# The input's additions in the down products: one pause more before and after each, and a buffer taken per block

## The chip, the cores and the metric

The kernel runs on one core of a Trainium2 chip. The metric is the device time of one execution, in microseconds. Five engines work side by side, each through its own queue in order: TensorE (PE) multiplies, VectorE (DVE), ScalarE (ACT) and GpSimd (POOL) work on elements, and SyncE (SP) starts the transfers. They wait for one another only through semaphores.

## The reference, cut to what matters

One layer of an encoder for 1104 tokens (64 of one request, 16 learned ones and 1024 of another) of width 1024. It begins and ends with half a feed-forward block, added to its own input:

```python
def half_ffn(x, g, wg, wu, wd):
    h = rmsnorm(x, g)
    return x + 0.5 * ((jax.nn.silu(h @ wg) * (h @ wu)) @ wd)

# in the layer, D_MODEL = 1024, D_FF = 2816
xp = half_ffn(xp, ffn1_norm[l], ffn1_wg[l], ffn1_wu[l], ffn1_wd[l])
...                      # DeltaNet heads and latent attention, each added to xp
xp = half_ffn(xp, ffn2_norm[l], ffn2_wg[l], ffn2_wu[l], ffn2_wd[l])
```

The change touches only how `x +` is done, in both blocks. "Down products" are those with `wd`, 2816 to 1024.

## The kernel before, in words

Activations lie transposed: 128 features on the partitions, 1104 tokens along the free dimension, cut for the products into pieces of 336, 384 and 384 (`CH`). A float32 factor is split into a high and a low part, and each product is three passes (high·high, high·low, low·high).

**The down products** (`down`, L968) take the 2816 inner features as 22 slices of 128, two at a time: ten groups of two in the main loop, the last two in another. Within a group the loop runs over the 8 blocks of 128 output features (`m`). A block is 2 slices x 3 passes x 3 pieces = 18 matmuls into three PSUM banks of the eight there are. When it is done, `evac` (L972) adds half of each bank to the result `R` in SBUF: for the first group ACT writes `R`, for all later ones DVE does three additions (`SCALAR_TENSOR_TENSOR R<-bk,R`). A bank is free for a new block when its addition is done.

Beside that run `down_loads` (rows of `wd` into `raw`, split by ACT and DVE into `wh`/`wl` or into two tiles both called `wx`) and `inner_loads` (two slices of inner activations from DRAM, split into pairs that the trace calls `st`, `XH`/`XL` or `ih`/`il`). Both fall at the start of a group: four casts on ACT, four subtractions on DVE.

**The input** `x` lies in DRAM as 8 blocks of 128x1104 (`x0`). `input_rows` (L1120) is a task of its own: for each `m` it loads the block into the tile `xa` and has DVE add it to `R`. There is one `xa`, so a load can start only when the addition before has read it.

**What sets the order.** The program is written by coroutines (`Tasks`, L430). Each `yield` gives the earliest modelled time of the next step (a number, counted from now) and what it needs: flags and free buffers. `step` picks the ready task of lowest rank, and the instructions go into each engine's queue in that order, for good. Times come from a small model (`Clock`), whose clock is TensorE's. `note` (L361) computes when an instruction would begin: from when its inputs are made, and, for a tile newly taken from a pool, from when the tile that had its place was last used. A tile that is merely written again has no such term. `nc.lag(xa)` is the modelled time until the load has landed. What the engines do at run time is set by the queues and by semaphores, which order load and addition on `xa` in either version.

`input_rows` waits for the flags `("R", m)` (`evac` of the first group has written block m) and `("R", m, 1)` (a later group has). It has rank 9, behind the products' helpers. All instructions are recorded under L424, the line of the helper that issues them, so tiles tell them apart.

Of the kernel before, what the change touches and what calls it, by code (L numbers as in the profile page):

```python
# [8 lines left out]
F32 = mybir.dt.float32  # L9
# [8 lines left out]
P = 128  # L18
# [6 lines left out]
T_ = NS + NM + NPR  # L25
# [784 lines left out]
def plain_steps(s, js, W, x, ready, tmp, hd, done):  # L810

    nc, T = s.nc, s.tasks
    V, A = nc.vector, nc.scalar
    hbs = []

    def gated(e, c, bs):
        yield 0, "sg"
        T.take("sg")
        t = tmp.tile([P, s.tw], F32, tag="sg", name="sg", bufs=CAPS["sg"])[:, :F]
        A.activation(t, bs[0][:, :F], AF.Silu)  # L820
        T.free("b")
        yield nc.lag(t), lambda: nc.complete(bs[1]) if len(bs) > 1 else None
        if not c:
            T.take("hb")
            hbs.append(tmp.tile([P, 2 * F], F32, tag="hb", name="hb", bufs=CAPS["hb"]))
        V.tensor_tensor(hbs[e][:, F * c:F * c + F], bs[1][:, :F], t, ALU.mult)
        T.free("b", "sg")
        if c:
            yield nc.lag(hbs[e])
            nc.sync.dma_start(hd[js[e]][:, :2 * F], hbs[e])  # L830
            T.free("hb", of=hbs[e])
            done.add((js[e], 0), nc.complete(hbs[e]) + 3.0)
    for c, e in [(0, 0), (0, 1), (1, 0), (1, 1)] + [(c, e) for e in js[2:] for c in (0, 1)]:
        bs = []
        for n in "AB":
            yield 0, "b", nc.when(W, (e, n))
            b = grab(s)
            for k in range(8):
                op = (0, 1, 7, 2)[2 * c + k // 4]
                if k % 4 == 0:  # L840
                    yield 0, ready.wait((0, op))
                mm3(nc, b[:, :F], [w[:, k * P:k * P + P] for w in W[e, n]], (x.h[op][:, k % 4, :], x.l[op][:, k % 4, :]), k == 0, k == 7)
            bs.append(b)
            if n == "A":
                T.add(gated(e, c, bs), -1)
        if c:
            T.free("A", "TS"[e % 2])
# [120 lines left out]
def down(s, R, fl, W, hs, free, last_group, after, chunks):  # L968

    nc, T = s.nc, s.tasks  # L970

    def evac(g, m, bs):  # L972
        for c, (o, w) in enumerate(CH):
            if g:
                nc.vector.scalar_tensor_tensor(R[:, m, o:o + w], bs[c][:, :w], 0.5, R[:, m, o:o + w], ALU.mult, ALU.add)
            else:
                nc.scalar.activation(R[:, m, o:o + w], bs[c][:, :w], AF.Copy, scale=0.5)
            T.free("b")
            yield 0
        fl.add(("R", m) + (1,) * (g > 0))  # L980

    def ready(j):
        return nc.when(W, j), nc.when(hs, j)
    for g in range(0, NF - 2, 2):
        for m in range(8):
            yield (0, "b", "b", "b", *ready(g), *ready(g + 1))
            bs = [grab(s) for c in range(3)]
            for i in (0, 1):
                for n, (x, y) in enumerate(PASSES):
                    for c, (o, w) in enumerate(CH):  # L990
                        nc.tensor.matmul(bs[c][:, :w], W[g + i][x][:, m, :], hs[g + i][y][:, o:o + w], start=(i + n == 0), stop=(i == 1 and n == 2))
                if not i:
                    yield 0
            T.add(evac(g, m, bs), -1)
        T.free(*free(g))
    last_group()
    g = NF - 2
    for c in chunks:
        o, w = CH[c]
        for m in range(8):  # L1000
            yield (0, "b", *ready(g), *ready(g + 1))
            b = grab(s)
            for i in (0, 1):
                mm3(nc, b[:, :w], [t[:, m, :] for t in W[g + i]], [t[:, o:o + w] for t in hs[g + i]], i == 0, i == 1)
            T.add(after(c, m, b), -1)


class Seven:
# [108 lines left out]
    def freed(self, g):  # L1117
        return ["d" + self.KINDS[j] for j in (g, g + 1)] + ["ix" if g // 2 % 2 else "is"]

    def input_rows(self, xa):  # L1120

        nc, T = self.s.nc, self.s.tasks
        for m in range(8):
            nc.sync.dma_start(xa, self.o.x0[m])
            yield nc.lag(xa), self.flags.wait(("R", m))
            nc.vector.tensor_tensor(self.R[:, m, :], self.R[:, m, :], xa, ALU.add)
            yield 0, self.flags.wait(("R", m, 1))
        self.flags.add("x0")

    def flow(self):  # L1130
        s, o, E = self.s, self.o, self.E
        nc, T = s.nc, s.tasks
        yield from plain_steps(s, range(o.plain), self.W1, o.x[0], o.ready, o.wk, self.hd, self.done)
        self.flags.add("plain")
        yield from half_steps(s, self.seq, self.W1, o.x, o.ready, o.wk, self.hd, self.done, {E - o.plain - 1: self.first_pair_done, E - 2: lambda: self.flags.add("last step", nc.at["tensor"])}, o.plain)
        yield 0, lambda: 0.0 if 1 in self.Wd else None
        o.second.close(1)
        o.first.close(1)
        pr = o.second("R")
        self.R = pr.tile([P, 8, T_], F32, name="R")  # L1140
        T.add(self.input_rows(pr.tile([P, T_], F32, name="xa")), 9)
        o.rest()

        def before_last():
            assert "x0" in self.flags
            T.free("w", "w", "w")
            o.before_last()
        yield from down(s, self.R, self.flags, self.Wd, self.hs, self.freed, before_last, o.after, o.chunks)
# [1105 lines left out]
def layer_kernel(tc, cst, x_prompt, x_sample, cache_mla_ckv, cache_mla_krope, state_gdn, state_conv, meta,  # L2254
# [21 lines left out]
    with ExitStack() as ctx:  # L2276
# [164 lines left out]
        def latents():  # L2441
# [24 lines left out]
            state.add("keys")  # L2466
        T.add(mix(), -2)
        T.add(flow(), 100)
        T.add(latents(), 99)
        for h in range(H):  # L2470
# [241 lines left out]
```

## Time and profile before

| | |
|---|---|
| three runs | 2384.83, 2392.31, 2393.76 us; median 2392.31 |
| the profiled execution | 2391.09 us, its span 2389.3 us |
| mean granted TensorE clock | 0.981 |
| first block's down products, main loop | from 515.5 us, 24.2 us a group when nothing waits |
| second block's down products | second group from 2113.49 us, third from 2137.69 us |


The profiled execution spends 1.8 us outside its span. A busy share says little here: PE is busy nearly everywhere, so what counts is where it stands still and where its clock is lower. The granted clock has two levels, 1.2 GHz (0.5) and 2.4 GHz (1.0); a stretch's figure is the mean over it.

### The profile page before, as it was taken

The page shows a single profiled execution, that of the slowest core. Times are in us where ns is not written, and L with a number is a line of the kernel's source. Part 1 is how long each engine was busy: PE and PEld are TensorE (multiplying, and loading weights), DVE is VectorE, ACT ScalarE, POOL GpSimd, SP SyncE. Part 2 cuts the span into 40 slices and gives each one's busy share as a digit, 9 for nine tenths or more (in the row PEclk, how much of TensorE's full clock was granted, in tenths as well). Part 3 has the DMA queues.
Part 4 walks back from the last instruction along what each step waited for, and adds up shares of the span by engine and source line. Part 5 has one row for each costly group of instructions (what it writes and reads, how often), then busy time and mean ns, then how long its engine had stood idle before and what let it go on. Part 6 is the DMA issues. An engine that isn't in the chain of part 4 may idle for free.

```text
span 2389.3 us, 41529 instructions
## 1 busy us (share of the span) xinstructions
PE 2306.6 (97%) x16356; PEld 2279.0 (95%) x16356; DVE 1511.5 (63%) x3499; ACT 925.2 (39%) x2038; POOL 203.7 (9%) x488
## 2 busy tenths in 40 slices
PE   9999999998999999899998999899999999989998
PEld 8999999998999899899998998899999999989998
DVE  7754455566666757878877566567554445747676
ACT  5333333351211445545633555334333333531123
POOL 0000000000000403322345000000000000000002
PEclk9999999998999999999998999999999999999999
DMA  6322222353230331112122103633222222453212
GB/s 197 117 75 78 82 82 71 100 200 122 79 114 28 115 88 49 54 36 64 37 69 66 48 17 95 194 106 99 82 65 72 82 83 84 139 182 103 81 55 76
DMA packets 231044, 214.30 MB, mean 90 GB/s; under 512 B 18372, under 2 KB 202864, under 8 KB 230848
## 3 DMA queue, kind: packets, MB, share of 16 engines
q1 hardware_dynamic: 230832, 211.64, 28.5%
q8 instruction: 128, 2.10, 0.4%
q14 instruction: 68, 0.56, 0.1%
q10 hardware_dynamic: 16, 0.00, 0.0%
HBM read 159.05 MB, written 52.55 MB: 89 GB/s over the span
## 4 chain that ended last, share of the span: by engine, by line
PE 82%; DVE 9%; DMA 3%; ACT 2%; issue 2%; POOL 1%; SPq 0%; DVEq 0%; POOLq 0%; ACTq 0%
PE bk L424 82%; DMA xa<-x 2%; DVE s L424 1%; DVE cv L424 1%; DVE R L424 1%; DVE wl L424 1%; DVE rs_q L424 1%; POOL rs_q L424 0%; DVE rs_r L424 0%; DMA X<-in_w_out_dram 0%; ACT s L424 0%; DMA s<-in_w_out_dram 0%; SPq L424 0%; POOL cql L424 0%; ACT wh L424 0%
## 5 line engine op out<-in xcount | busy, mean ns | idle before, releaser
L424 PE MATMUL bk<-s,wh 128*128 128x276 f32 x3136 | 601.1, 290 | 5.1 <-ACT sn L424 2.4
L424 PEld LDWEIGHTS bk<-s,wh 128*128 128x128 f32 x3136 | 493.2, 188 | 6.5 <-ACT sn L424 2.6
L424 PE MATMUL bk<-s,wl 128*128 128x276 f32 x1568 | 449.3, 290 | 1.6 <-DVE wl L424 1.6
L424 PE MATMUL bk<-s,wx 128*128 128x276 f32 x2964 | 394.0, 290 | 1.7 <-DVE s L424 1.7
L424 PEld LDWEIGHTS bk<-s,wx 128*128 128x128 f32 x2964 | 383.5, 188 | 1.9 <-DVE s L424 1.9
L424 DVE SCALAR_TENSOR_TENSOR R<-bk,R 128x384 f32<-128x384 f32 (+1 forms) x480 | 230.7, 533 | 131.7 <-PE bk L424 130.6
L424 PEld LDWEIGHTS bk<-s,wl 128*128 128x128 f32 x1568 | 293.5, 188 | 2.1 <-DVE wl L424 2.1
L424 DVE TENSOR_TENSOR sn<-bk,sn 128x276 f32<-128x276 f32 x237 | 105.0, 444 | 205.6 <-PE bk L424 201.7
L424 ACT COPY sn<-bk 128x276 f32<-128x276 f32 x237 | 91.9, 389 | 243.7 <-PE bk L424 240.7
L424 PE MATMUL bk<-XH,wh 128*128 128x384 f32 (+1 forms) x576 | 166.5, 343 | 0.0
L424 PE MATMUL bk<-XL,wh 128*128 128x384 f32 (+1 forms) x576 | 161.3, 334 | 0.0
L424 PE MATMUL bk<-XH,wl 128*128 128x384 f32 (+1 forms) x576 | 161.2, 334 | 0.0
L424 DVE TENSOR_TENSOR raw<-wx,raw 128x512 f32<-128x512 f32 x40 | 27.7, 691 | 157.5 <-DMA raw<-in_ffn_wu_dram 157.5
L424 ACT CAST wh<-wx 128x512 fp32r<-128x512 f32 (+1 forms) x89 | 76.4, 858 | 101.4 <-DVE wx L424 88.0
L424 DVE TENSOR_TENSOR wx<-raw,wx 128x512 fp32r<-128x512 f32 (+2 forms) x149 | 112.0, 755 | 2.9 <-ACT wx L424 2.8
L424 ACT ACTIVATE sn<-sn 128x276 f32<-128x276 f32 x158 | 68.5, 435 | 116.5 <-DVE sn L424 116.4
L424 PEld LDWEIGHTS bk<-XH,wh 128*128 128x128 f32 x576 | 105.5, 191 | 0.0
L424 PEld LDWEIGHTS bk<-XL,wh 128*128 128x128 f32 x576 | 105.5, 191 | 0.0
L424 PEld LDWEIGHTS bk<-XH,wl 128*128 128x128 f32 x576 | 105.3, 191 | 0.0
L424 DVE TENSOR_TENSOR wl<-raw,wh 128x512 fp32r<-128x512 f32 (+4 forms) x95 | 89.7, 947 | 13.4 <-ACT wh L424 13.4
L424 ACT CAST wh<-raw 128x512 fp32r<-128x512 f32 (+4 forms) x95 | 77.2, 815 | 52.6 <-PE bk L424 28.7
L424 DVE TENSOR_TENSOR wl<-wx,wh 128x512 fp32r<-128x512 f32 (+1 forms) x89 | 87.1, 979 | 12.4 <-ACT wh L424 12.4
(436 smaller groups left out, 4476.1 us busy)
## 6 DMA issues: line engine op xcount, KB each, us to landing
raw<-in_ffn_wu_dram SPq DMA_DIRECT2D x102, 256.0 KB, 4.6
wx<-in_ffn_wg_dram SPq DMA_DIRECT2D x49, 512.0 KB, 4.1
hd<-hb SPq DMA_DIRECT2D x88, 276.0 KB, 2.1
raw<-in_ffn_wd_dram SPq DMA_DIRECT2D x40, 512.0 KB, 4.3
XH<-hd SPq DMA_DIRECT2D x24, 552.0 KB, 3.6
XL<-hd SPq DMA_DIRECT2D x20, 552.0 KB, 4.5
xa<-x SPq DMA_DIRECT2D x16, 552.0 KB, 3.6
raw<-in_w_in_dram SPq DMA_DIRECT2D x16, 512.0 KB, 3.9
```

The costliest lines, as they stand in the source:

```text
L424: r = f(*args, **kw)
```

## The change

`input_rows` gets the pool instead of a tile, and takes `xa` from it for each block. The earliest time of the addition becomes the modelled landing plus 6 us, and that of the next load 6 us after the addition.

```diff
-    def input_rows(self, xa):
+    def input_rows(self, pool):
 
         nc, T = self.s.nc, self.s.tasks
         for m in range(8):
+            xa = pool.tile([P, T_], F32, tag="xa", name="xa")
             nc.sync.dma_start(xa, self.o.x0[m])
-            yield nc.lag(xa), self.flags.wait(("R", m))
+            yield nc.lag(xa) + 6.0, self.flags.wait(("R", m))
             nc.vector.tensor_tensor(self.R[:, m, :], self.R[:, m, :], xa, ALU.add)
-            yield 0, self.flags.wait(("R", m, 1))
+            yield 6.0, self.flags.wait(("R", m, 1))
         self.flags.add("x0")
...
-        T.add(self.input_rows(pr.tile([P, T_], F32, name="xa")), 9)
+        T.add(self.input_rows(pr), 9)
```

The pool holds one buffer for the tag `xa`, so it is the same memory as before. The queues of PE, ACT and POOL keep their order in the whole program; DVE's and SP's change in the two phases of down products alone.

DVE's queue in the first feed-forward block, from the middle of the second group on, before (`R<-R,xa` is an addition of the input, `R<-bk,R` of 128x336 and the two of 128x384 are one block's evacuation, `XL` and `wx` are splits of the next group):

```order
L424 SCALAR_TENSOR_TENSOR R<-bk,R 128x336
L424 SCALAR_TENSOR_TENSOR R<-bk,R 128x384 x2
L424 TENSOR_TENSOR R<-R,xa 128x1104 x2
L424 SCALAR_TENSOR_TENSOR R<-bk,R 128x336
L424 SCALAR_TENSOR_TENSOR R<-bk,R 128x384 x2
L424 TENSOR_TENSOR R<-R,xa 128x1104 x2
L424 SCALAR_TENSOR_TENSOR R<-bk,R 128x336
L424 SCALAR_TENSOR_TENSOR R<-bk,R 128x384 x2
L424 TENSOR_TENSOR XL_6042<-XL_5709,XH_6041 128x1104
L424 TENSOR_TENSOR wx_6045<-raw,wx_6044 128x1024
L424 SCALAR_TENSOR_TENSOR R<-bk,R 128x336
L424 SCALAR_TENSOR_TENSOR R<-bk,R 128x384 x2
```

The same place with the change, from the last block of the second group on:

```order
L424 SCALAR_TENSOR_TENSOR R<-bk,R 128x336
L424 SCALAR_TENSOR_TENSOR R<-bk,R 128x384 x2
L424 TENSOR_TENSOR XL_6033<-XL_5708,XH_6032 128x1104
L424 TENSOR_TENSOR R<-R,xa 128x1104
L424 TENSOR_TENSOR wx_6036<-raw,wx_6035 128x1024
L424 SCALAR_TENSOR_TENSOR R<-bk,R 128x336
L424 SCALAR_TENSOR_TENSOR R<-bk,R 128x384 x2
L424 TENSOR_TENSOR XL_6033<-XL_5708,XH_6032 128x1104
L424 TENSOR_TENSOR wl<-raw,wh 128x1024
L424 SCALAR_TENSOR_TENSOR R<-bk,R 128x336
L424 SCALAR_TENSOR_TENSOR R<-bk,R 128x384 x2
```

Two pairs of additions, each pair in direct sequence, are gone from between the evacuations; one addition stands among the next group's splits, ahead of the evacuations of its first two blocks. The eight additions of a feed-forward block stand in two groups before (the last four of them in the rows shown) and in six with the change. The same holds for the second block, where one addition stands behind all four splits of a group:

```order
L424 TENSOR_TENSOR XL_23691<-XL_23466,XH_23690 128x1104
L424 TENSOR_TENSOR wx_23694<-raw,wx_23693 128x1024
L424 SCALAR_TENSOR_TENSOR R<-bk,R 128x336
L424 SCALAR_TENSOR_TENSOR R<-bk,R 128x384 x2
L424 TENSOR_TENSOR XL_23691<-XL_23466,XH_23690 128x1104
L424 TENSOR_TENSOR wl<-raw,wh 128x1024
L424 TENSOR_TENSOR R<-R,xa 128x1104
L424 SCALAR_TENSOR_TENSOR R<-bk,R 128x336
L424 SCALAR_TENSOR_TENSOR R<-bk,R 128x384 x2
```

There the addition moved from the run before the splits to just before the second block's evacuation.

SP's queue at the same place of the first block, before (`xa<-x` loads the input, `XH`/`XL` the inner slices, `raw` rows of `wd`):

```order
L424 DMA xa<-x_119 128x1104
L424 DMA raw<-in_ffn_wd_dram 128x1024
L424 DMA xa<-x_119 128x1104 x2
L424 DMA XH_5925<-hd_128 128x1104
L424 DMA XH_5925<-hd_129 128x1104
L424 DMA xa<-x_119 128x1104 x4
L424 DMA raw<-in_ffn_wd_dram 128x1024
L424 DMA XL_6129<-hd_130 128x1104
```

And with the change:

```order
L424 DMA xa<-x_119 128x1104
L424 DMA raw<-in_ffn_wd_dram 128x1024
L424 DMA XH_5906<-hd_128 128x1104
L424 DMA XH_5906<-hd_129 128x1104
L424 DMA xa<-x_119 128x1104
L424 DMA raw<-in_ffn_wd_dram 128x1024
L424 DMA XL_6121<-hd_130 128x1104
L424 DMA XL_6121<-hd_131 128x1104
L424 DMA xa<-x_119 128x1104
L424 DMA raw<-in_ffn_wd_dram 128x1024 x2
L424 DMA xa<-x_119 128x1104
L424 DMA XH_6339<-hd_132 128x1104
```

The six loads that stood close together are one or two a group now, with the group's other loads between them.

## Rows read from the trace of the kernel before

**Rows 1.** The page: busy time by engine, and the chain's lines.
```profile
PE 2306.6 (97%) x16356; PEld 2279.0 (95%) x16356; DVE 1511.5 (63%) x3499; ACT 925.2 (39%) x2038; POOL 203.7 (9%) x488
PE bk L424 82%; DMA xa<-x 2%; DVE s L424 1%; DVE cv L424 1%; DVE R L424 1%; DVE wl L424 1%; DVE rs_q L424 1%; POOL rs_q L424 0%; DVE rs_r L424 0%; DMA X<-in_w_out_dram 0%; ACT s L424 0%; DMA s<-in_w_out_dram 0%; SPq L424 0%; POOL cql L424 0%; ACT wh L424 0%
```

**Rows 2.** Waits of the span: engine and line, releaser, total us, times, longest.
```profile
DVE R L424 <- DMA xa<-x: 28.5, 12, 3.7
...
PE bk L424 <- DVE R L424: 17.5, 5, 6.6
```

**Rows 3.** Stretches by group: length; busy of PE, PEld, DVE, ACT, POOL; PEclk.
```profile
539.84:565.66 25.82, 24.45 (x145) 24.15 (x145) 17.14 (x25) 4.18 (x6) 0.00 (x0) 1.00 0.41 135
565.66:603.13 37.47, 30.04 (x145) 29.27 (x145) 21.42 (x35) 4.02 (x4) 0.00 (x0) 0.82 0.29 101
603.13:627.32 24.19, 24.19 (x146) 24.19 (x145) 16.11 (x29) 4.03 (x4) 0.00 (x0) 1.00 0.26 91
2113.49:2137.69 24.20, 24.20 (x146) 24.20 (x145) 17.31 (x27) 4.17 (x6) 0.00 (x0) 1.00 0.53 189
2137.69:2174.69 37.00, 28.29 (x146) 27.68 (x146) 20.92 (x35) 4.02 (x4) 0.00 (x0) 0.86 0.32 105
```

**Rows 4.** Timeline of PE, both phases: start, us, instruction, idle before.
```profile
554.95 0.49 PE L424 MATMUL bk<-XH,wx 128*128 128x336 f32 x2
556.81 0.45 PE L424 MATMUL bk<-XH,wx 128*128 128x384 f32 x1 [1.37 <-DVE R L424]
...
569.44 2.53 PE L424 MATMUL bk<-st,wx 128*128 128x384 f32 x7 [3.28 <-DVE R L424]
...
579.48 2.53 PE L424 MATMUL bk<-st,wx 128*128 128x384 f32 x7 [4.15 <-DVE R L424]
...
2147.80 2.53 PE L424 MATMUL bk<-ih,wx 128*128 128x384 f32 x7 [6.60 <-DVE R L424]
...
2155.26 2.12 PE L424 MATMUL bk<-ih,wx 128*128 128x384 f32 x7 [2.11 <-DVE R L424]
```

**Rows 5.** Timeline of DVE in the second and third group, first phase.
```profile
544.89 1.29 DVE L424 TENSOR_TENSOR R<-R,xa 128x1104 f32<-128x1104 f32 x1
546.11 1.30 DVE L424 TENSOR_TENSOR st<-XH,st 128x1104 fp32r<-128x1104 f32 x1
...
554.84 1.31 DVE L424 TENSOR_TENSOR R<-R,xa 128x1104 f32<-128x1104 f32 x1 [2.08 <-DMA xa<-x]
556.25 2.78 DVE L424 SCALAR_TENSOR_TENSOR R<-bk,R 128x336 f32<-128x336 f32 x6
...
567.65 1.31 DVE L424 TENSOR_TENSOR R<-R,xa 128x1104 f32<-128x1104 f32 x1 [3.74 <-DMA xa<-x]
568.88 1.43 DVE L424 SCALAR_TENSOR_TENSOR R<-bk,R 128x336 f32<-128x336 f32 x3
572.49 1.31 DVE L424 TENSOR_TENSOR R<-R,xa 128x1104 f32<-128x1104 f32 x1 [2.19 <-DMA xa<-x]
```

**Rows 6.** Timeline of SP in the second and third group, first phase.
```profile
556.17 17.97 SPq L424 DMA_DIRECT2D xa<-x  x4
```

**Rows 7.** The tile xa: DVE's additions (ns), and its transfers.
```profile
L424 DVE TENSOR_TENSOR R<-R,xa x16: 1295/1308/1309, 521.9 to 2151.1; 128x1104 f32<-128x1104 f32 x16
...
DMA to landing us min/median/max: 3.5/3.6/6.7
```

**Rows 8.** Timeline of DVE around the undisturbed group that starts at 603.13.
```profile
602.98 1.44 DVE L424 SCALAR_TENSOR_TENSOR R<-bk,R 128x336 f32<-128x336 f32 x3 [1.57 <-PE bk L424]
604.48 1.31 DVE L424 TENSOR_TENSOR st<-XH,st 128x1104 fp32r<-128x1104 f32 x1
605.71 1.22 DVE L424 TENSOR_TENSOR wx<-raw,wx 128x1024 fp32r<-128x1024 f32 x1
606.85 1.43 DVE L424 SCALAR_TENSOR_TENSOR R<-bk,R 128x336 f32<-128x336 f32 x3
...
610.54 2.96 DVE L424 SCALAR_TENSOR_TENSOR R<-bk,R 128x336 f32<-128x336 f32 x6
615.09 1.44 DVE L424 SCALAR_TENSOR_TENSOR R<-bk,R 128x336 f32<-128x336 f32 x3 [1.58 <-PE bk L424]
```

## The prediction

> **What bounds the kernel now.** First the page: PE is busy for 97% of the span and 82% of the chain of work that ended last is matmuls, so time is won only where PE stands still or runs at half clock [rows 1]. One entry of that chain does not fit a loop of products: 2% of the span, near 48 us of 2389.3, is loads of `xa` [rows 1]. The table of waits says how these reach PE: DVE stood 28.5 us in 12 additions until `xa` had landed, and PE stood 17.5 us in 5 places until DVE had evacuated banks, the longest 6.60 us [rows 2, 4].
>
> The two phases of down products, cut at their groups, show what that costs. A group with nothing in its way takes 24.19 us at clock 1.00; the second and third of the first phase take 25.82 and 37.47, the third of the second phase 37.00, with PE's five gaps in them and clocks of 0.82 and 0.86 in the two long ones [rows 3, 4]. In each stretch 145 or 146 matmuls are recorded, so it is the same work [rows 3].
>
> DVE's timeline tells why. With one `xa`, a load starts when the addition before has read it; the load lands 3.5 us later at the least, 3.6 at the median, 6.7 at the most [rows 7]. The additions stand so close in DVE's queue that there is nothing between two of them that lasts as long. So DVE stops at one addition (567.65, after 3.74 us idle), evacuates one block, and stops again at 572.49 after 2.19 us [rows 5]. SP's queue shows the same from the other side: four loads of `xa` in sequence take from 556.17 to 574.14, each one sent when the addition before it is done [rows 6].
>
> **The change part by part.**
>
> *What it removes.* The additions stand in six groups instead of two, the loads likewise. If no addition then stops DVE, each phase gets back what its groups took above 24.19 us [rows 3]: first phase (25.82 - 24.19) + (37.47 - 24.19) = 1.63 + 13.28 = 14.91 us; second phase 0.01 + 12.81 = 12.82. Together 27.73 us. Of it 17.51 us are the five gaps: 1.37, 3.28, 4.15, 6.60, 2.11 [rows 4]. The other 10.2 us are matmuls at the lower of the two clock levels, which set in after the longer gaps: 0.82 over 37.47 us is 6.7 us less full clock, 0.86 over 37.00 us 5.2 us, part of it inside the gaps [rows 3]. Both parts go together, since no gap is then left to lower the clock.
>
> *What it moves onto DVE's tight places.* The additions themselves, 16 of 1.31 us each, stay [rows 7]; in sequence one holds the queue for 546.11 - 544.89 = 1.22 us [rows 5]. In an undisturbed group DVE idles 1.57 us a block [rows 8], so behind the fourth block's evacuation an addition hides. At a group's start it is different: four splits come with the evacuations, and in six places (three a phase) an addition now stands among them, ahead of the second block's evacuation. From the group that starts at 603.13: blocks last 24.19 / 8 = 3.02 us and end at 606.15 and 609.18; their evacuations start at 606.85 and 610.54, so 0.70 and 1.36 us late [rows 3, 8]. With an addition ahead these become 1.92 and 2.58 us. How late may they be? At 554.95 PE began a block, issued two matmuls and waited for its third bank until 556.81, when the evacuation that started at 556.25 had freed a bank after its first piece, 0.56 us [rows 4, 5]. That block's second predecessor had just ended one block, 3.02 us, before 554.95. So an evacuation must start by 3.02 + 0.33 (the two matmuls: 336 + 384 of the block's 6 x 1104 columns) - 0.56 = 2.79 us after its block's end. 2.58 is inside by 0.21 us. I cost these six places at nothing. If the margin is missed, each costs at least a sliver and, by the smallest gap seen, up to 1.37 us: 8.2 us in all. The third block's evacuation is nearer again (0.9 us late by the same steps), so it does not add up.
>
> *The loads' place in SP's queue.* Each addition has 6 us more than the modelled landing ahead of it. The least room is where the load is sent when a group's first weight split has freed a buffer and the addition stands behind the fourth evacuation: in the group of rows 8 that is from 606.85 to 615.09 + 1.34 = 616.43, 9.6 us, and 1.22 less where an addition pushes the splits: 8.4. The longest landing was 6.7 [rows 7]. So no addition waits, by 1.7 us at least. SP itself is held less, since an addition is long done when the next load comes up; what stands behind (rows of `wd`, inner slices) is used a group, 24 us, later. Cost nothing; were a load late by a microsecond or two, DVE has the 1.58 us of that block [rows 8] and PE does not feel it.
>
> The Trainium skill speaks against such mixing: its page "DMA: Bandwidth & Descriptors", section "Queues, rings and completion order", says that each DMA engine takes the descriptors of one issuing engine in ring order, so that an `xa` sent right behind rows of `wd` would wait for these. If that load too took the longest landing seen and `xa` its 3.6 behind it, it would land after 10.3 us, 1.9 us after its addition's turn; one evacuation would start that much later than now, still within its 2.79 us, and the sum would be the same. What it would change is the margin, and with it the second rival's chance.
>
> *The buffer taken anew.* One buffer per tag, so the same wait of load for addition as before; the only effect is on the modelled times. Nothing by itself.
>
> *What is late next.* With DVE out of the way PE is bound by its own matmuls through both phases, as in the groups at 24.19 us. PE's other waits lie in stages whose order doesn't change, and they move earlier by the same time. Gains below the sum are bounded by the 8.2 us; more than the sum can only come from half-clock stretches elsewhere falling differently, some 2 us either way by the size of those above.
>
> **The sum.** Against the profiled execution, 2391.09 - 27.7 = 2363.4 us; the median of the runs is 1.2 us above it, so 2364.6. I say 2364.
>
> **The rivals.**
>
> *Late evacuations at the group starts take part of it back.* For it: six places with 0.21 us of margin. Against it: the gaps seen needed a whole load's wait. All six at 1.37 us: 2364 + 8 = 2372. Chance 0.07.
>
> *The additions still stop DVE.* One `xa` remains, and if a load were held in SP's queue until its addition's turn, the wait only moves. For it: waiting loads took 18 us of SP's queue in one go [rows 6]. Against it: 8.4 us of room against 6.7. If each phase kept its loss: 2392, no change. Chance 0.03.
>
> *Slower: six gaps instead of five.* The place is the same six group starts; it decides at the 2.79 us. Were each of the six to open a gap as dear as those of now, with the clock lost behind it, that is 14.91 / 3 = 5.0 us in the first phase and 12.82 / 2 = 6.4 in the second: 3 x 5.0 + 3 x 6.4 = 34.2 us against 27.7 won, so 2392 + 6.5 = 2398. For it: a late evacuation is exactly what opens the gaps now. Against it: the dear gaps are 2 to 6.6 us long, and one addition is 1.22.
> The Trainium skill makes this rival dearer than its idle time: "TensorE: Matmul & The Clock Gate", section "HAM oscillation — how this bites in real kernels", says that waits which recur between bursts of matmuls put the clock back each time and that the return is paid once per wait. The trace agrees for the long gaps (0.82, 0.86 [rows 3]); behind the 1.37 us gap the stretch keeps 1.00 [rows 3, 4], so by the row six short gaps are 8.2 us and by the rule 34. Chance 0.02, since it needs gaps of a length that a single addition cannot make.
>
> **How the numbers follow.** Forecast 0.88, the partial rival 0.07, no effect 0.03, slower 0.02. A difference of 0.5%, 12 us, is about what a measurement of this kernel can tell from no change. Faster by more (under 2380): forecast and partial rival, 0.95; within 0.5%: 0.03; slower: 0.02. The runs before lay from 7.5 below their median to 1.5 above; I take 7 us below the forecast for that, and above it the partial rival's 8: 2357 to 2372, which leaves out some 2 in 10.
>
> **What would show it right or wrong.** Right: every group of both phases but the first near 24.2 us at clock 1.00; no wait of PE for DVE's `R` in them; DVE's 28.5 us of waiting for `xa` near nothing; the 2% of `xa` gone from the chain. The margin: second evacuations of the six groups about 2.6 us after their block, and PE without gap. Wrong in the sum: groups of 25 us or more where an addition stands among the splits, or additions that still wait for their load. Wrong altogether: PE's gaps in as many places as now, or the clock below 1.00 in these phases.

## The result

The changed kernel takes 2363.38 us (median of 4 runs, 2361.39 to 2365.06) against 2390.80 (4 runs, 2384.83 to 2393.76): a ratio of 0.9888, 95% interval 0.9866 to 0.9910, so 27.4 us or 1.1% less. The forecast was 2364 us, with a range of 2357 to 2372. The profiled execution went from 2391.09 to 2365.06 us.

The page of the changed kernel, busy time and the chain's lines, answers to [rows 1]:

```profile
PE 2299.7 (97%) x16356; PEld 2273.8 (96%) x16356; DVE 1511.4 (64%) x3499; ACT 926.4 (39%) x2038; POOL 204.3 (9%) x488
...
PE bk L424 85%; DVE s L424 1%; DVE cv L424 1%; DVE wl L424 1%; DVE rs_q L424 1%; DMA X<-in_w_out_dram 1%; DVE rs_r L424 0%; ACT wh L424 0%; POOL rs_q L424 0%; ACT s L424 0%; DMA s<-in_w_out_dram 0%; DVE st L424 0%; ACT pp L424 0%; POOL tkq L424 0%; DMA wx<-in_ffn_wg_dram 0%
```

DVE did the same work in the same time (1511.4 us against 1511.5). The loads of `xa` are gone from the chain, and matmuls fill 85% of it where they filled 82%.

The stretches by group, to be read beside [rows 3]: the second, third and fourth group of the first phase, the second and third of the second.

```profile
540.92:565.09 24.17, 24.17 (x145) 24.17 (x145) 14.91 (x26) 4.17 (x6) 0.00 (x0) 1.00 0.26 93
565.09:589.14 24.05, 24.05 (x145) 24.05 (x145) 17.23 (x30) 4.03 (x4) 0.00 (x0) 1.00 0.31 115
589.14:613.32 24.18, 24.18 (x145) 24.18 (x145) 18.44 (x31) 4.03 (x4) 0.00 (x0) 1.00 0.39 138
2100.39:2124.59 24.20, 24.20 (x145) 24.20 (x145) 14.90 (x26) 4.17 (x6) 0.00 (x0) 1.00 0.38 139
2124.59:2148.70 24.11, 24.11 (x145) 24.11 (x145) 17.23 (x30) 4.03 (x4) 0.00 (x0) 1.00 0.34 115
```

PE is busy for the whole of each group and its clock is 1.00. Against before the groups are shorter by 25.82 - 24.17 = 1.65, 37.47 - 24.05 = 13.42 and 37.00 - 24.11 = 12.89: 27.96 us. (Undisturbed groups alternate between 24.05 and 24.18 us in the first phase and 24.11 and 24.20 in the second; the prediction took 24.19 for all, hence its 27.73.) The two profiled spans differ by 26.0, since in this pair of executions the stages ahead of the first phase (its first group starts at 516.60 instead of 515.5) and between the phases were a microsecond longer each.

PE's waits of the whole span, longest first: the entry of 17.5 us for DVE's `R` [rows 2], which led the list, is not in it.

```profile
PE bk L424 <- ACT s L424: 5.2, 2, 4.1
PE bk L424 <- POOL qt L424: 5.1, 3, 3.5
PE bk L424 <- DVE Tpg L424: 5.1, 3, 2.9
```

The tile `xa` in the changed kernel. Under the two headings on waiting there is no line; before, 28.5 us of DVE's waiting for `xa` stood there.

```profile
L424 DVE TENSOR_TENSOR R<-R,xa x16: 1296/1299/1309, 527.1 to 2213.4; 128x1104 f32<-128x1104 f32 x16
its engine sat idle before it (us, times) until:
who waited for it (us, times):
...
DMA to landing us min/median/max: 3.4/5.3/7.1
```

The landing times are a thin sample: the trace kept the landing of two of the sixteen loads, 7.1 us for the first (sent at 513.33, ahead of the phase) and 3.4 us for the one sent at 606.91, and the 5.3 lies between these two. The 3.5, 3.6 and 6.7 of [rows 7] are three landings in the same way, the 6.7 that of the first load. So it is not shown that loads land later than before.

The six groups of a phase that hold additions now include the phase's first one. Counted in the same way there were three before, with one, four and three additions, not two.

### The profile page after: what moved, and what is told of

It reads as the page before. It is cut to its first block, busy times and chain, and to the rows that moved or that the text cites. A ratio compares the mean times of both kernels' runs of the same rounds, so it can differ in the third digit from the quotient of the medians.

```text
span 2363.3 us, 41362 instructions
## 1 busy us (share of the span) xinstructions
PE 2299.7 (97%) x16356; PEld 2273.8 (96%) x16356; DVE 1511.4 (64%) x3499; ACT 926.4 (39%) x2038; POOL 204.3 (9%) x488
## 4 chain that ended last, share of the span: by engine, by line
PE 85%; DVE 9%; ACT 2%; DMA 2%; issue 1%; POOL 1%; SPq 0%; DVEq 0%; ACTq 0%; POOLq 0%
PE bk L424 85%; DVE s L424 1%; DVE cv L424 1%; DVE wl L424 1%; DVE rs_q L424 1%; DMA X<-in_w_out_dram 1%; DVE rs_r L424 0%; ACT wh L424 0%; POOL rs_q L424 0%; ACT s L424 0%; DMA s<-in_w_out_dram 0%; DVE st L424 0%; ACT pp L424 0%; POOL tkq L424 0%; DMA wx<-in_ffn_wg_dram 0%
```

## The experiments

The theory: PE lost its time because DVE, whose queue is in order, stopped at additions whose one tile was not loaded yet, with evacuations queued behind them; the changed order leaves a load its time. The rivals: SP's queue, held by these loads, was what cost; additions that stand close together cost by themselves; one of the two edits does nothing; and, on the price, that late evacuations at the group starts are as dear as the gaps of before. Beside the runs `e1` to `e4` the kernel before took 2390.95 us (13 runs), beside `e5` to `e7`, on another chip, 2392.90 (7 runs). Undisturbed groups repeat to 0.02 us from kernel to kernel, so a group's length shows small losses even in a single run.

**Each edit alone.** `e1_anew`, the tile taken anew, without pauses:

```diff
         for m in range(8):
+            xa = pool.tile([P, T_], F32, tag="xa", name="xa", bufs=1)
             nc.sync.dma_start(xa, self.o.x0[m])
             yield nc.lag(xa), self.flags.wait(("R", m))
...
```

> The buffer taken anew for each block, without the two pauses. In the model a load now begins only when the addition before has ended, so the additions stand 2 to 4 blocks apart, 6 to 12 us, instead of 1 to 2. Theory (time went into DVE stopping at additions whose load had not landed): a load needs 3.6 us, 6.7 at most, so hardly any stop is left: 2363 to 2366 us, DVE's wait for xa under 3 us. Rival (it is the 6 us pauses that bring the gain, and the buffer does nothing): 2388 to 2394 us, as before.

`e2_pauses`, the pauses without the tile taken anew:

```diff
-            yield nc.lag(xa), self.flags.wait(("R", m))
+            yield nc.lag(xa) + 6.0, self.flags.wait(("R", m))
             nc.vector.tensor_tensor(self.R[:, m, :], self.R[:, m, :], xa, ALU.add)
-            yield 0, self.flags.wait(("R", m, 1))
+            yield 6.0, self.flags.wait(("R", m, 1))
```

> The two pauses of 6 us with the one tile of before. Theory: the additions stand 5 or more blocks apart in the queue, no load is late: 2362 to 2365 us, the same as with the whole change. Rival (the buffer taken anew brings part of the gain): 2370 to 2392 us.

Measured: 2363.89 us (ratio 0.9887, 0.9873 to 0.9902) and 2361.44 (0.9878, 0.9860 to 0.9897). Each edit brings all of it, and both together no more. In `e1_anew` the whole of phase one and two is free of gaps too, here its second and third groups:

```profile
543.97:568.14 24.17, 24.17 (x145) 24.17 (x145) 17.33 (x28) 4.18 (x6) 0.00 (x0) 1.00 0.35 116
568.14:592.19 24.05, 24.05 (x145) 24.05 (x145) 18.54 (x31) 4.04 (x4) 0.00 (x0) 1.00 0.47 162
```

So my sentence that the tile taken anew does "nothing by itself" was wrong as it stood. At run time a load waits for the same addition as before, but the model that writes the order then knows that a load follows the addition before, and that alone sets the additions, from a phase's second one on, three or four evacuations apart in DVE's queue, where there were none to three. The pauses do the same by hand.

This run also bears on SP's queue. It still stood for `xa` for 21.5 us (33.1 in the kernel before), and the gain is whole:

```profile
SPq L424 <- DMA xa<-x: 21.5, 8, 3.3
```

**Two tiles, order as before.** `e3_two`:

```diff
+            xa = xas[m % 2]
             nc.sync.dma_start(xa, self.o.x0[m])
...
-        T.add(self.input_rows(pr.tile([P, T_], F32, name="xa")), 9)
+        T.add(self.input_rows([pr.tile([P, T_], F32, name=n) for n in ("xa", "xb")]), 9)
```

> The kernel before, its additions and loads where they were in the queues, with two tiles used in turn, so that a load waits only for the addition before the last. Theory (what costs is the wait for the load, not that additions stand close together): loads run one ahead, most of DVE's 28.5 us of waiting goes, PE's gaps fall from 17.5 us to under 5: 2363 to 2372 us. Rival (additions that stand close delay the evacuations by themselves, and have to be spread): DVE's wait goes but PE's gaps stay near 15 us, 2385 to 2392 us.

Measured: 2365.33 us (0.9890, 0.9874 to 0.9907). The additions still stand where they stood, partly in pairs. With loads one ahead DVE waits 3.2 us in all for `xa` and `xb`, and PE's gaps in both phases are these three:

```profile
569.44 1.45 PE L424 MATMUL bk<-st,wx 128*128 128x384 f32 x7 [0.92 <-DVE R L424]
573.14 1.45 PE L424 MATMUL bk<-st,wx 128*128 128x384 f32 x7 [0.42 <-DVE R L424]
2131.39 1.45 PE L424 MATMUL bk<-ih,wx 128*128 128x384 f32 x7 [0.88 <-DVE R L424]
```

That sets the two causes apart: 2.2 us of gaps are left of 17.5, so it is the wait for the load that cost and not how close the additions stand. By the groups' lengths, 25.94 and 25.27 us, 1.9 and 1.2 above the changed kernel's, 3.1 us are left of 28. How much of these 3.1 goes to the waits that remain, and how much to the pairs, is not shown.

**SP's queue free.** `e4_pool` sends the loads from the queue of an engine with nothing to do in these phases:

```diff
-            nc.sync.dma_start(xa, self.o.x0[m])
+            nc.gpsimd.dma_start(xa, self.o.x0[m])
```

> The kernel before, with the loads of xa sent from POOL's queue, which is empty in these phases, instead of SP's. The additions stay where they were. Theory: DVE still stops at each addition for a whole load, 28 us or more in all: 2389 to 2396 us, no gain. Rival (SP's queue, held up to 18 us by these loads with rows of wd and inner slices behind them, was what PE paid for): SP is free now, 2363 to 2370 us.

Measured: 2393.84 us (10 runs; 1.0010, 1.0000 to 1.0019). SP no longer waits for `xa`; POOL does:

```profile
POOL xa L424 <- DVE R L424: 117.7, 13, 24.7
DVE R L424 <- DMA xa<-x: 30.5, 12, 3.9
PE bk L424 <- DVE R L424: 19.8, 10, 3.5
```

The additions did not quite stay where they were, as the expectation had it: in the trace of this run one addition stands between each two evacuations of those blocks, and the pairs are gone. So the run changes two things. But DVE stops as often as before and as long (12 times, 30.5 us against 28.5), PE has ten shorter gaps instead of five (19.8 us against 17.5), and no time is won. With `e1_anew`, where SP's queue was held and the gain was whole, the queue that sends the loads is out as the cause.

**The price of a late evacuation.** `e5_twice` puts a second instruction of the same length behind each addition, by the engine's own call, which the planning model does not see, so the order stays the changed kernel's:

```diff
             nc.vector.tensor_tensor(self.R[:, m, :], self.R[:, m, :], xa, ALU.add)
+            nc.nc.vector.tensor_tensor(xa, xa, xa, ALU.add)
```

> The changed kernel with a second DVE instruction of the same length (xa added to itself, not used) behind each of the 16 additions, all else in the order of the changed kernel. In the six tight places the second block's evacuation then starts 2.58 + 1.22 = 3.80 us after its block. Theory (limit 2.79 us, short gaps cost their idle time alone): six gaps of 1.0 us, 6 us more than the changed kernel: 2368 to 2371 us. Rival (the dear gaps: each lowers the clock behind it and costs 5 to 6.4 us): 34 us more, 2395 to 2400 us. Rival (the limit is wider than read, PE does not notice): 2362 to 2365 us.

Measured: 2373.89 us (0.9922, 0.9898 to 0.9946). That is 10.5 us above the changed kernel, but the kernel before is 2.1 us slower on this chip too; against it the gain is 19.0 us instead of 27.4, so 8.4 less. This is more than the first theory's 6, and far from the rival's 34. The six groups are 25.24 to 25.39 us long, at clock 1.00; the one between, where the addition stands behind the second evacuation, has lost nothing:

```profile
565.01:590.39 25.38, 24.63 (x145) 24.04 (x145) 18.55 (x31) 4.03 (x4) 0.00 (x0) 1.00 0.30 109
590.39:615.64 25.25, 24.72 (x145) 24.13 (x145) 20.98 (x33) 4.03 (x4) 0.00 (x0) 1.00 0.39 132
615.64:639.69 24.05, 24.05 (x145) 24.05 (x145) 18.45 (x31) 4.04 (x4) 0.00 (x0) 1.00 0.34 115
639.69:664.93 25.24, 24.72 (x146) 24.12 (x145) 20.89 (x33) 4.03 (x4) 0.00 (x0) 1.00 0.30 109
2130.11:2155.50 25.39, 24.40 (x146) 24.10 (x146) 18.55 (x31) 4.03 (x4) 0.00 (x0) 1.00 0.33 109
```

That is 1.33 + 1.07 + 1.05 in the first phase and, by the same cut, 1.28 + 1.04 + 1.05 in the second: 6.8 us, against the 6 forecast. The profiled execution is 8.9 us longer than the changed kernel's; the other 2 lie in the stage between the phases (1320.4 us against 1318.2). That stage is not edited; it took from 1314 to 1322 us in the profiles of the kernels here, and why it was long in this one is open.

How the loss shows is worth a look. PE's own waits for the evacuations are half of the 6.8 us; those of the weight loads (PEld) are about all of it:

```profile
PEld bk L424 <- DVE R L424: 7.1, 11, 1.3
...
PE bk L424 <- DVE R L424: 3.4, 7, 1.0
```

`e6_sweep` does the same with shorter instructions in the six places alone:

```diff
+            n = {2: (100, 200), 3: (300, 500), 6: (700, 900)}.get(m, (0, 0))[self.o.plain == 4]
+            if n:
+                nc.nc.vector.tensor_tensor(xa[:, :n], xa[:, :n], xa[:, :n], ALU.add)
```

> The changed kernel with a second, shorter DVE instruction behind the addition in the six tight places alone, of 100, 300 and 700 columns in the first phase and 200, 500 and 900 in the second: by the 1.22 us of 1104 columns about 0.13, 0.35, 0.79 and 0.24, 0.57, 1.0 us. Theory (limit 2.79 us, margin 0.21): PE's gap at these places is the addition's length less 0.21 us: 0, 0.14, 0.58 and 0.03, 0.36, 0.8 us. Rival (limit wider): no gaps at the short ones and the line starts later. Rival (the margin is nil): gaps from the shortest on.

One run, 2365.74 us. DVE at the first place, in the group from 565.82 (the instruction of 100 columns stands between addition and `wx`), and four of the groups:

```profile
568.40 1.30 DVE L424 TENSOR_TENSOR R<-R,xa 128x1104 f32<-128x1104 f32 x1
569.74 0.26 DVE L1130 TENSOR_TENSOR xa<-xa 128x100 f32<-128x100 f32 x1
569.92 1.22 DVE L424 TENSOR_TENSOR wx<-raw,wx 128x1024 fp32r<-128x1024 f32 x1
```

```profile
565.82:590.12 24.30, 24.30 (x145) 24.02 (x145) 17.50 (x31) 4.03 (x4) 0.00 (x0) 1.00 0.32 114
590.12:614.55 24.43, 24.43 (x145) 24.17 (x145) 18.93 (x32) 4.03 (x4) 0.00 (x0) 1.00 0.39 136
638.62:663.46 24.84, 24.49 (x146) 24.19 (x145) 19.24 (x32) 4.03 (x4) 0.00 (x0) 1.00 0.31 111
2123.63:2148.08 24.45, 24.41 (x146) 24.10 (x146) 17.61 (x31) 4.03 (x4) 0.00 (x0) 1.00 0.33 113
```

What an inserted instruction adds is read from the starts: here 569.92 - 568.40 = 1.52 instead of 1.22, so 0.30 us; the group is 24.30 - 24.05 = 0.25 longer, so the margin was 0.05. The other places by the same reading: added 0.50 and 0.92, lost 0.25 and 0.66 in the first phase; added 0.40, 0.72, 1.14, lost 0.34, 0.43, 0.83 in the second. The margin is 0.05 us in the two places where the addition stands behind a split. It is 0.25 to 0.31 in the four where the addition stands before the group's first split: there the changed kernel's second evacuation starts only 2.43 us after its block (at 597.61 in the group from 589.14), not 2.62. Both rivals are half right; a margin of 0.21 everywhere was not.

`e7_long` makes long gaps in four of the places:

```diff
+            for i in range({2: (2, 5), 3: (0, 0), 6: (3, 4)}.get(m, (0, 0))[self.o.plain == 4]):
+                nc.nc.vector.tensor_tensor(xa, xa, xa, ALU.add)
```

> The changed kernel with 2 and 3 more DVE instructions of 1.22 us behind the addition in two tight places of the first phase, and 5 and 4 in two of the second, so gaps of 2.2, 3.5, 5.9 and 4.7 us by the limit of 2.79. What it measures is the price of a gap by its length: groups of 24.19 us plus idle time, plus what the lower clock costs. Theory: the gap of 2.2 us costs little more than itself and those from 3.5 us on another 1.5 to 3.5 us each, as in the kernel before (10.2 us over five gaps); the whole 16 us of gaps and 4 to 10 us of lower clock: 2384 to 2390 us. Rival (the clock falls with any of these waits, whatever their length): each group pays 3.4 us and more on top.

One run, 2389.36 us. PE's gaps, and the four groups in the same order:

```profile
573.81 1.45 PE L424 MATMUL bk<-st,wx 128*128 128x384 f32 x7 [1.68 <-DVE R L424]
577.51 1.46 PE L424 MATMUL bk<-st,wx 128*128 128x384 f32 x7 [0.40 <-DVE R L424]
...
649.92 0.45 PE L424 MATMUL bk<-XH,wx 128*128 128x384 f32 x1 [2.80 <-DVE R L424]
653.62 0.44 PE L424 MATMUL bk<-XH,wx 128*128 128x384 f32 x1 [0.40 <-DVE R L424]
...
2151.03 2.53 PE L424 MATMUL bk<-ih,wx 128*128 128x384 f32 x7 [6.36 <-DVE R L424]
...
2226.27 0.69 PE L424 MATMUL bk<-XH,wx 128*128 128x384 f32 x1 [4.13 <-DVE R L424]
```

```profile
565.63:592.33 26.70, 24.62 (x145) 24.03 (x145) 19.86 (x32) 4.04 (x4) 0.00 (x0) 1.00 0.29 104
640.56:668.51 27.95, 24.75 (x146) 24.14 (x145) 22.29 (x34) 4.03 (x4) 0.00 (x0) 1.00 0.28 99
2135.14:2167.26 32.12, 25.76 (x145) 25.46 (x145) 23.77 (x35) 4.03 (x4) 0.00 (x0) 0.89 0.26 86
2215.57:2245.51 29.94, 25.81 (x146) 25.51 (x145) 23.59 (x35) 4.03 (x4) 0.00 (x0) 0.94 0.25 92
```

Behind the gaps of 1.68 and 2.80 us, each followed by one of 0.40, the clock stays at 1.00. Their groups are 2.65 and 3.77 us longer, 0.6 more than the gaps listed; as in `e5_twice` the rest is waiting that shows at the weight loads, whose busy time stays at 24.03 and 24.14 us. Behind 4.13 us the group's clock is 0.94, behind 6.36 it is 0.89. These groups are 5.7 and 8.0 us longer, 1.6 more than their gaps, and of that 1.3 us is slower work: the weight loads are busy for 25.51 and 25.46 us.

The four lose 20.2 us, at the low end of the theory's 20 to 26. The rival that any of these waits lowers the clock falls. The theory was wrong in one place: the gap planned as 3.5 us, measured as 2.80 and 0.40, paid nothing for the clock. The whole run is 24.3 us above the changed kernel's profiled execution, as the unedited stage between the phases was 3.6 us longer in it.

## Why the prediction was right, point by point

**The sum.** 27.73 us were to come back; the three groups gave 27.96, the medians 27.4. It held because it was not built from the waits (17.5 us) but from whole groups against an undisturbed one, which has the lower clock in it. That no gap would be left to lower the clock is what the groups at 1.00 show. That the median came within a microsecond of the forecast is partly luck: the runs spread over 3.7 us, and the profiled execution fell by 26.0.

The split of the sum into 17.5 us of gaps and 10.2 us of lower clock was off, though nothing hung on it. In the kernel before, too, the weight loads show more of the waiting than the matmuls:

```profile
PEld bk L424 <- DVE R L424: 19.2, 5, 6.9
```

Their busy time in the two long groups of [rows 3] is 29.27 and 27.68 us instead of 24.19, which leaves 8.6 us to the lower clock.

**The cause.** That DVE stopped for loads, and not how close the additions stand, was argued from [rows 5] and is now shown: two tiles with the old order keep only 2.2 us of the gaps (`e3_two`), a free SP queue wins nothing (`e4_pool`), and one held for 21.5 us costs nothing (`e1_anew`).

**The loads' room.** No addition waited, as forecast. There was more room than the 8.4 us of the prediction: the shortest time from sending a load to its addition was 11.1 us (642.64 to 653.70), as the addition stands behind the group's fifth evacuation and not its fourth. The Trainium skill ("DMA: Bandwidth & Descriptors", "Queues, rings and completion order") has each DMA engine consume descriptors in ring order; the prediction drew from it that a load waits for those sent before it. The runs do not show whether this happened: two kept landings cannot tell, and with 11.1 us of room nothing came of it.

**The tight places, costed at nothing.** Right in the sum, but in two of the six places much closer than it said. In the changed kernel DVE's queue at the start of such a group reads:

```profile
566.44 1.31 DVE L424 TENSOR_TENSOR XL<-XL,XH 128x1104 fp32r<-128x1104 f32 x1
567.67 1.30 DVE L424 TENSOR_TENSOR R<-R,xa 128x1104 f32<-128x1104 f32 x1
568.89 1.22 DVE L424 TENSOR_TENSOR wx<-raw,wx 128x1024 fp32r<-128x1024 f32 x1
570.02 1.43 DVE L424 SCALAR_TENSOR_TENSOR R<-bk,R 128x336 f32<-128x336 f32 x3
571.37 1.30 DVE L424 TENSOR_TENSOR XL<-XL,XH 128x1104 fp32r<-128x1104 f32 x1
...
573.72 2.77 DVE L424 SCALAR_TENSOR_TENSOR R<-bk,R 128x336 f32<-128x336 f32 x6
```

The second block ended at 565.09 + 24.05 / 4 = 571.10, so its evacuation is 2.62 us late where I had 2.58. With 0.05 us of margin measured there, the limit is 2.67 and not 2.79: the step from one stall of [rows 4, 5] to the limit was 0.12 us too wide. The same stall gives 2.67 if it is priced by its group: the evacuation at 556.25 came 4.32 us after its block's end (554.95 - 3.02), and the group lost 1.65 us. The gap of 1.37 us that PE showed was less than what it cost.

**The slower rival.** Its mechanism exists: an evacuation past the limit opens a gap. Its price was about five times too high, as the groups of `e5_twice` lost 1.05 to 1.33 us each and not 5 to 6.4. On the Trainium skill's rule that recurring waits put the clock back ("TensorE: Matmul & The Clock Gate", "HAM oscillation — how this bites in real kernels"): it shows in `e7_long` behind gaps of 4.13 and 6.36 us, and not in `e5_twice` behind six losses of about 1 us that stand a group or more apart.

**The tile taken anew.** Costed at nothing by itself, and in this the working failed: alone it is worth the whole gain (`e1_anew`). The number did not suffer, since the two edits do not add up; that was luck.

## What to carry to other kernels

Here a load into a single buffer made its consumer a stop in an in-order queue, because the consumers stood closer together than the transfer lasts; what was paid for was all that is queued behind the stop. Moving the consumers apart took the stop away, a second buffer took away nearly all of it (28 us lost before, 3.1 with it); one of the two was enough. Where a planner writes the order, look first at whether its model knows that writing a buffer again waits for its last reader. Price such a stall by the whole stretch against an undisturbed one, not by PE's idle time: short waits showed only in part as PE's gaps, and behind long ones the clock was lower.

## What the runs showed of the hardware that was not expected

A DVE instruction that writes `xa` right behind the addition that reads it starts 1.33 or 1.34 us after the addition, in all 16 places of `e5_twice`; one that uses neither of its tiles starts after 1.21 to 1.23 us. The lines are 568.40 and 569.74 in `e6_sweep`, 567.67 and 568.89 in the changed kernel. In its record the dependent one waits for DVE's own semaphore.

The lower clock did not come with long gaps alone. In `e4_pool` ten gaps of 0.70 to 3.49 us cost 29 us, with the clock of their four groups at 0.94 and 0.95. In the second of these groups there are two gaps, 5.4 us apart; below them stands the group's stretch:

```profile
576.37 1.46 PE L424 MATMUL bk<-st,wx 128*128 128x384 f32 x7 [2.09 <-DVE R L424]
581.75 1.99 PE L424 MATMUL bk<-st,wx 128*128 128x384 f32 x7 [2.09 <-DVE R L424]
```

```profile
573.79:604.14 30.35, 26.17 (x145) 25.58 (x145) 20.12 (x34) 4.02 (x4) 0.53 (x1) 0.94 0.26 92
```

The fourth group, with gaps of 2.14 and 2.24 us, reads the same. In `e7_long` a gap of 2.80 us with one of 0.40 behind it left the clock at 1.00. So the longest gap of a stretch does not settle it; what does is not shown here.
